# Hymba-style layer on one core: the channel mixer's sums go from GpSimd to VectorE, with new orders in its first blocks, its last token tile and its banks

## The chip, the cores and the metric

One core of one Trainium2 chip runs the whole layer as one program. The metric is the device time in microseconds (us) from launch to end; the profiled execution's span runs from the first to the last instruction. The engines are named as in the profile: PE is TensorE (matmul), DVE is VectorE, ACT is ScalarE, POOL is GpSimd, SP is SyncE, which issues nearly all DMA transfers.

## The reference

```python
def conv_glu(h, w_up, conv_w, conv_b, w_down):
    a, val = jnp.split(h @ w_up, 2, axis=-1)
    a = jax.nn.gelu(dwconv(a, conv_w, conv_b))        # depthwise, width 3, centred
    return (a * val) @ w_down
...
        x = x + g_a * (jnp.concatenate([y_m, y_a], axis=-1) @ w_out[l])
        x = x + g_f * conv_glu(modulate(rmsnorm(x, norm_ffn[l]), sh_f, sc_f),
                               w_up[l], ffn_conv_w[l], ffn_conv_b[l], w_down[l])
    return rmsnorm(x, final_norm)
```

One layer (DEPTH 1) over 1024 latent tokens of width 1024, with 256 context tokens ahead. Before the lines above come the adaLN-modulated norm, one input projection, a bidirectional mLSTM of 4 heads and windowed attention of 8 heads; the change does not touch these. The channel mixer has a width of 2816, all in fp32.

## The kernel before

Every fp32 product is split in two: an operand is copied to a rounded high part (fp32r, on ACT) and a low part is made by subtracting the high part from the operand (on DVE). A product is then three matmuls: high by high, high by low, low by high. The functions `split2`, `split`, `wsplit` and `cut` make such pairs; in the profile they are tiles such as `wh`/`wl` (up weights), `hB` (both parts of the activations, `hB[0]` and `hB[1]`), `dh`/`dl` (down weights) and `ah`/`al` (down activations).

The two large products of the channel mixer use a Strassen-Winograd form: seven block products in place of eight, at the price of sums of blocks before and after. In the up projection the activations (token halves by model halves) and each block's weights (value and gate columns by model halves) form 2 by 2 blocks. The activation sums T1 to T4 are made once, per token tile, by `sum1`, `sum2` and `sum34`. The weight sums are made for every block of 128 columns: `sums_v` makes `R[1][2]` and `R[1][3]`, `sums_g` makes `R[1][1]` and `R[1][4]`, from the four raw blocks that `load_R` brings as two transfers into Ra (2 blocks) and Rb (2 blocks and room for 3 sums).

The work in order, with the stretch of the span:

- Out-projection of the second half and the norm, up to about 683 us. Token tiles are taken in the order 1, 5, 2, 6, 3, 7, 4. `trans` turns a tile by PE into banks of the pool pT, `evac` brings it to SBUF with the modulation (tile `raw`; `er` for tile 4), and `split`, `sum1`, `sum2`, `sum34` and `split34` make the mixer's operands in `hB`. The finished x tile is stored to `x2_d` by SP.
- First products. `ps_a` (`pa`) and `ps_a2` use the weights `e0` loaded early. The five others of block 0 are `ps0` f, c, b, e, d (`pf` and so on), with `wB`, `wS`, `wA` for their weights.
- 22 blocks of the up projection (`blocks`, in pairs j and j + 11). Block 0 is made from `ps0`. For each later block PE does seven products of 12 matmuls, in the order a, b, A, c, e, d, C; A adds to the bank of a, C to the bank of c. `sn_` copies a to SBUF before A adds to its bank; `u2_`, `av2`, `av1` and `vt_` add the Winograd sums out of the banks; C can add to the bank of c when `av2` has read it. `ident_`, `taps`, `gelu` are the depthwise convolution and its activation, `mul1` (DVE) and `mul2` (POOL) the product with the value half, `combine` (POOL) the activation sums of the down projection, which SP stores to DRAM (`act_a`, `act_s`). The loop body for block i works on C = block i in PE and finishes B = block i - 1. The weights of block i + 1 are split in the meantime: `split_w(0)` to `split_w(3)` call `wsplit`, for products a/A, b/c, e/d and C. `Ra` and `Rb` have one buffer each, so their next load waits until they are read.
- Down projection: seven products m1, m6, m2, m7, m5, m4, m3 of 11 steps by 4 token tiles, the steps in pairs (`PAIRS`). `load` starts transfers four steps ahead (raw weights `br`, `b`; activations `ar`), `cut` splits them two steps ahead, and between them stand weight sums on POOL and DVE. After each product `after` adds the four results into `us`, `vs` and the output rows `os_`, one per step (`todo`).
- Tail: the last four token tiles are finished one by one and stored.

From the out-projection on, PE, DVE, ACT and POOL run their instructions in the order in which the program has them (`tc.manual_schedule`, the `fence`); SP joins after the first products (`sp_order`). Each engine takes its own list in order, so an instruction that waits holds all that stand behind it on that engine.

A helper shows its own line in the profile: `sub` is L1189, `add` L1354, `prod` L1282, the copy of `wsplit` L1377, the two halves of `split2` L1172 and L1173, `split`'s copy L1255, `dprod` L1752. So many groups share a line and are told apart by their tiles.

## Time and profile before

| | |
|---|---|
| median of 3 runs | 1367.38 us (1363.44 to 1367.88) |
| profiled execution | 1370.23 us, span 1368.4 us, mean granted PE clock 0.979 |
| busy share of the span | PE 94%, DVE 73%, ACT 44%, POOL 36% |
| DMA | 171.42 MB, mean 125 GB/s |

How to read the profile: a group is told by its line, engine, operation and tiles (out<-in), with its count, its busy time, the mean of one in ns and the idle time ahead of it with what ended that wait. The chain is followed back from the last instruction, at each step to what released it. The granted clock is what the throttle gave PE; at 0.5 a matmul of 512 columns takes 0.43 us from start to start instead of 0.23. Rows of a stretch give busy times and counts for PE, PEld (weight loads), DVE, ACT and POOL, then the clock, the DMA share and GB/s.

### The profile page before, as it was taken

What the parts mean: (1) busy time and instruction counts of PE and PEld (TensorE: products, weight loads), DVE (VectorE), ACT (ScalarE), POOL (GpSimd) and SP (SyncE); (2) the same over time, 40 slices, a digit from 0 to 9 for tenths busy, and PEclk for the clock granted to TensorE, in tenths of its full rate; (3) what the DMA queues carried; (4) which work ended last, traced back from release to release, by engine and by line L of the source; (5) the groups of instructions that cost most, each with busy time, mean ns of one, the idle gap of its engine ahead of it and who ended that gap; (6) DMA issues with size and microseconds to landing.
All of it is one profiled execution on the core that took longest, in us unless ns stands there. A gap on an engine that the chain in (4) does not pass through costs nothing.

```text
span 1368.4 us, 19850 instructions
## 1 busy us (share of the span) xinstructions
PE 1285.2 (94%) x7141; PEld 1085.3 (79%) x7141; DVE 998.1 (73%) x1736; ACT 605.7 (44%) x1195; POOL 492.9 (36%) x471
## 2 busy tenths in 40 slices
PE   6889999999898999999978999999999999899997
PEld 4689898999898777788756888777777878788786
DVE  4644787876675788996878676677667676887778
ACT  6532344444565566776644233223232333343445
POOL 0440131413445223332343444434344442535080
PEclk9999999999999999999989999999999999999999
DMA  9430443330035312212412333332332326884654
GB/s 360 150 109 32 139 143 120 121 119 5 33 98 186 134 63 84 82 67 73 156 64 77 115 94 107 100 89 88 116 100 87 114 93 222 277 314 139 223 162 154
DMA packets 86018, 171.42 MB, mean 125 GB/s; under 512 B 12672, under 2 KB 25120, under 8 KB 85920
## 3 DMA queue, kind: packets, MB, share of 16 engines
q1 hardware_dynamic: 85920, 170.16, 37.4%
q8 instruction: 56, 0.92, 0.3%
q14 instruction: 42, 0.34, 0.1%
HBM read 131.84 MB, written 38.29 MB: 124 GB/s over the span
## 4 chain that ended last, share of the span: by engine, by line
PE 27%; DVE 19%; DMA 7%; issue 7%; ACT 5%; POOL 1%; SPq 1%; ACTq 0%; DVEq 0%; POOLq 0%
PE pd L1752 9%; DVE wl L1189 4%; DMA Rb<-in_w_up_dram 3%; DMA act_s<-tt 3%; PE pa L1282 2%; PE pc L1282 2%; PE u L1069 2%; DVE tt L1472 2%; DVE tt L1474 2%; PE po L297 2%; PE pb L1282 2%; PE po L299 1%; PE po L298 1%; DVE al L1173 1%; ACT tt L1478 1%
## 5 line engine op out<-in xcount | busy, mean ns | idle before, releaser
L1752 PE MATMUL pd<-dh,al 128*128 128x512 f32 x296 | 116.5, 393 | 5.5 <-DVE al L1173 5.4
L1282 PE MATMUL pc<-hB,wh 128*128 128x512 f32 x344 | 109.4, 400 | 10.1 <-DVE av L1354 10.0
L1752 PE MATMUL pd<-dh,ah 128*128 128x512 f32 x296 | 115.9, 391 | 0.8 <-ACT ah L1172 0.8
L1752 PE MATMUL pd<-dl,ah 128*128 128x512 f32 x296 | 115.9, 392 | 0.0
L1282 PE MATMUL pa<-hB,wh 128*128 128x512 f32 x336 | 104.3, 392 | 3.9 <-ACT sn L1448 3.7
L1189 POOL TENSOR_TENSOR Rb<-Ra,Rb 128x512 f32<-128x512 f32 x44 | 71.7, 1649 | 92.4 <-DVE Rb L1354 92.3
L1189 DVE TENSOR_TENSOR wl<-Rb,wh 128x1024 fp32r<-128x1024 f32 (+1 forms) x65 | 100.0, 1587 | 6.7 <-ACT wh L1377 6.7
L1464 ACT ACTIVATE tt<-av,sp 128x1024 f32<-128x1024 f32 x22 | 27.4, 1245 | 165.5 <-DVE av L1354 62.7
L1282 PEld LDWEIGHTS pc<-hB,wh 128*128 128x128 f32 x344 | 64.2, 191 | 30.1 <-DVE av L1354 17.0
L536 PE MATMUL pp<-hl,wh 128*128 128x512 f32 x256 | 79.8, 403 | 0.0
L1282 PEld LDWEIGHTS pa<-hB,wh 128*128 128x128 f32 x336 | 62.5, 188 | 19.6 <-ACT sn L1448 6.9
L659 POOL TENSOR_SCALAR dm<-ident,mh 128x128 fp32r<-128x128 f32 x64 | 30.2, 473 | 131.7 <-PE pe L666 91.1
L297 PE MATMUL pv<-wh,hl 128*128 128x256 f32 x256 | 74.9, 292 | 0.0
L298 PE MATMUL pv<-wl,hl 128*128 128x256 f32 x256 | 72.3, 282 | 0.0
L299 PE MATMUL pv<-wh,hl 128*128 128x256 f32 x256 | 72.2, 282 | 0.0
L1752 PEld LDWEIGHTS pd<-dh,al 128*128 128x128 f32 x296 | 55.9, 189 | 18.8 <-DVE al L1173 7.4
L1484 POOL TENSOR_TENSOR tt<-vt,tt 128x512 f32<-128x512 f32 x22 | 31.0, 1407 | 108.3 <-ACT tt L1478 63.9
L1282 PE MATMUL pc<-hB,wl 128*128 128x512 f32 x172 | 67.6, 393 | 0.0
L1752 PEld LDWEIGHTS pd<-dh,ah 128*128 128x128 f32 x296 | 56.0, 189 | 12.8 <-ACT ah L1172 1.2
L1173 DVE TENSOR_TENSOR al<-ar,ah 128x1024 fp32r<-128x1024 f32 (+1 forms) x37 | 66.0, 1783 | 0.1
L1282 PE MATMUL pa<-hB,wl 128*128 128x512 f32 x168 | 65.4, 389 | 0.0
L1752 PEld LDWEIGHTS pd<-dl,ah 128*128 128x128 f32 x296 | 55.9, 189 | 12.0
(1076 smaller groups left out, 4056.6 us busy)
## 6 DMA issues: line engine op xcount, KB each, us to landing
w<-in_w_ada_dram SPq DMA_DIRECT2D x64, 256.0 KB, 2.8
br<-in_w_down_dram SPq DMA_DIRECT2D x25, 512.0 KB, 5.8
Ra<-in_w_up_dram SPq DMA_DIRECT2D x22, 512.0 KB, 3.6
Rb<-in_w_up_dram SPq DMA_DIRECT2D x22, 512.0 KB, 4.5
ar<-act_s SPq DMA_DIRECT2D x44, 256.0 KB, 3.0
act_a<-tt SPq DMA_DIRECT2D x33, 256.0 KB, 4.9
act_s<-tt SPq DMA_DIRECT2D x33, 256.0 KB, 5.1
wr<-in_w_h_dram SPq DMA_DIRECT2D x16, 512.0 KB, 4.8
```

The costliest lines, as they stand in the source:

```text
L297: T.matmul(ps, st_hi, mv_hi, start=first, stop=False)
L298: T.matmul(ps, st_hi, mv_lo, start=False, stop=False)
L299: T.matmul(ps, st_lo, mv_hi, start=False, stop=last)
L536: T.matmul(pp[:, 512 * n:512 * n + 512], wkq[sw][:, kt, cs], hl[n][part][:, kt, :], start=kt == 0 and sw + part == 0, stop=kt == KT - 1 an ...
L659: G.tensor_scalar(out=dm[:, d], in0=ident[:], scalar1=mhf[:, d, c, h:h + 1], scalar2=1.0, op0=ALU.mult, op1=ALU.mult)
L1069: T.matmul(self.u[:], vv[:, c, self.g], part[i][:, kk * 2 * P:(kk + 1) * 2 * P], start=kb + m == 0, stop=kb == last and m == 1)
L1173: V.tensor_tensor(out=lo, in0=src, in1=hi.bitcast(F32), op=ALU.subtract)
L1189: sub = lambda e, o, x, y: e.tensor_tensor(out=o, in0=x, in1=y, op=ALU.subtract)
L1282: T.matmul(ps[:], wt[sw][:, j, ks], hB[part][:, blk, kt, :], start=first and kt == 0 and sw + part == 0, stop=last and kt == 3 and sw == 1 ...
L1464: S.activation(self.tt[:], self.av[:], AF.Identity, bias=self.w(3), scale=self.w(1))
L1484: G.tensor_tensor(out=self.tt[:, h2_], in0=self.vt[:], in1=self.tt[:, h2_], op=ALU.mult)
L1752: T.matmul(ps[:], ac[sa][:, js], w[sw], start=first and n == 0, stop=last and n == 2, skip_group_check=not fresh)
```

## The change

The change has these parts.

1. Last token tile (4): it is turned in two halves with a product (`ps_a2`) between them and evacuated in two halves; its x store is issued by ACT. `split34` now copies at once and returns the subtractions; those of the last pair before it run after the norm's reciprocal.
2. First products: POOL makes all four weight sums of block 0; the split `wS` subtracts on DVE; the sums T3 and T4 of the last two tiles go from POOL to DVE and each is followed by its split.
3. Banks: pT opens on the other side, and the pool of six shared banks for b, c, e, d becomes two for f and b (`pB`) and four for c, e, d (`pC`).
4. Blocks: `sums_g` goes to DVE. Blocks 0 and 1 get an order of their own ahead of and in the first turn of the loop. In the other turns `sums_v` and `split_w(0)` stand after `u2_`, `av2` right behind them, and `sums_g`, `split_w(1)`, `split_w(2)` after `av2`, `split_w(3)` after `ident_`. The load of Ra is issued by itself ahead of that of Rb.
5. Down projection: the weight sums on POOL go to DVE, with the add one step later; the multiply-adds of `after_m2` and `after_m5` that ran on POOL go to DVE, the one of `after_m2` into a new `after_m7`.
6. Tail: the first half of the last tile's output is issued by ACT.

The diff; "..." stands where unchanged lines are left out:

```diff
 DB = 2
+RB1 = 1
 RB = 4
...
     pTk = ExitStack()
-    pT = pTk.enter_context(tc.tile_pool(name="pT2", bufs=4, space=PSUM, reuse_waits="tile"))
+    pT = pTk.enter_context(tc.tile_pool(name="pT2", bufs=4, space=PSUM, side="right", reuse_waits="tile"))
     pOk = ExitStack()
...
-    def trans(b):
+    def trans(b, kts=None):
         w = 2 if b == 4 else 4
-        pts[b] = [pT.tile([P, 4, P], F32, name="pt", tag="t") for _ in range(KT // w)]
-        if b == 4:
-            pts[b] = pts[b][2:] + pts[b][:2]
-        for kt in (4, 5, 6, 7, 0, 1, 2, 3) if b == 4 else range(KT):
+        if not kts:
+            pts[b] = [pT.tile([P, 4, P], F32, name="pt", tag="t") for _ in range(KT // w)]
+        else:
+            pts.setdefault(b, [None] * 4)
+            for i in sorted({kt // 2 for kt in kts}):
+                pts[b][i] = pT.tile([P, 4, P], F32, name="pt", tag="t")
+        for kt in kts or range(KT):
             T.transpose(pts[b][kt // w][:, kt % w], hns[b][:, kt * P:(kt + 1) * P], ident[:])
-    def evac(b):
+    def evac(b, kts=None):
         w = KT // len(pts[b])
-        raws[b] = (tbp.tile([P, 2, 4, P], F32, name="raw00") if b == 0 else
-                   er[:].rearrange("p a (k t) -> p a k t", k=4) if b == 4 else
-                   tbp.tile([P, 2, 4, P], F32, name="raw", tag=f"raw{b // 4}", bufs=2 - b // 4))
-        for kt in (4, 5, 6, 7, 0, 1, 2, 3) if b == 4 else range(KT):
+        if b not in raws:
+            raws[b] = (tbp.tile([P, 2, 4, P], F32, name="raw00") if b == 0 else
+                       er[:].rearrange("p a (k t) -> p a k t", k=4) if b == 4 else
+                       tbp.tile([P, 2, 4, P], F32, name="raw", tag=f"raw{b // 4}", bufs=RB1 if b > 4 else 2))
+        for kt in kts or range(KT):
             ga, sh = ada2[:, 16 + kt:17 + kt], ada2[:, 8 + kt:9 + kt]
...
+    def sum3(b, e=V):
+        sub(e, raws[b][:, 0], raws[b][:, 1], raws[b][:, 0])
+    def sum4(b, e=V):
+        sub(e, raws[b - 4][:, 1], raws[b - 4][:, 1], tbs[b][:, 0])
     def sum34(b):
-        sub(G, raws[b][:, 0], raws[b][:, 1], raws[b][:, 0])
-        sub(G, raws[b - 4][:, 1], raws[b - 4][:, 1], tbs[b][:, 0])
+        sum3(b, G)
+        sum4(b, G)
...
     def split34(b):
-        split(V, b, T3, 1, raws[b][:, 0:1])
-        split(V, b, T4, 1, raws[b - 4][:, 1:2])
+        parts = [(raws[b][:, 0:1], T3), (raws[b - 4][:, 1:2], T4)]
+        ts = slice(b % 4 * P, b % 4 * P + P)
+        for src, blk in parts:
+            S.copy(hB[0][:, blk:blk + 1, :, ts], src)
+        def lo():
+            for src, blk in parts:
+                sub(V, hB[1][:, blk:blk + 1, :, ts], src, hB[0][:, blk:blk + 1, :, ts].bitcast(F32))
+        return lo
...
         if late and b != last:
-            late()
+            late()()
             late = None
...
             split_t2(pp)
-        nc.sync.dma_start(x2_d[b][:], xs[b])
+        if b != last:
+            nc.sync.dma_start(x2_d[b][:], xs[b])
         if i + 2 < len(order):
...
     prod(ps_a, e0, 0, B11, True, True)
-    late()
+    lo = late()
     sq(4, 1)
     norm_b(4, True)
+    lo()
+    nc.scalar.dma_start(x2_d[4][:], xs[4])
     evac(7)
-    trans(4)
+    trans(4, (4, 5, 6, 7))
+    ps_a2 = pA.tile([P, 512], F32, name="pa2", tag="a")
+    prod(ps_a2, e0, 1, B21, True, True)
+    trans(4, (0, 1, 2, 3))
     pOk.close()
+    pB = pu.enter_context(tc.tile_pool(name="pB", bufs=2, space=PSUM, reuse_waits="tile"))
     pb_.close()
...
-    def load_R(m):
-        R = fr.tile([P, 2, 512], F32, name="Ra", tag="Ra"), fr.tile([P, 5, 512], F32, name="Rb", tag="Rb")
-        for t in range(2):
+    def load_R(m, ts=(0, 1), R=None):
+        R = R or [fr.tile([P, 2 + 3 * t, 512], F32, name=f"R{'ab'[t]}", tag=f"R{t}") if t in ts else None for t in range(2)]
+        for t in ts:
+            R[t] = R[t] or fr.tile([P, 2 + 3 * t, 512], F32, name=f"R{'ab'[t]}", tag=f"R{t}")
             nc.sync.dma_start(R[t][:, 0:2], I["w_up"][m, :, 2 * t:2 * t + 2].rearrange("p q k f -> p q (k f)"))
...
-    def sums_g(R, n):
-        if n == 0:
-            sub(G, R[1][:, 1], R[0][:, 0], R[1][:, 1])
-        else:
-            sub(G, R[1][:, 4], R[0][:, 1], R[1][:, 3])
+    def sums_g(R, e=V):
+        sub(e, R[1][:, 4], R[0][:, 1], R[1][:, 3])
+        sub(e, R[1][:, 1], R[0][:, 0], R[1][:, 1])
...
     sums_v(R, G)
-    sums_g(R, 1)
-    ps_a2 = pA.tile([P, 512], F32, name="pa2", tag="a")
-    prod(ps_a2, e0, 1, B21, True, True)
+    sums_g(R, G)
+    evac(4, range(4, 8))
+    sum1(7)
     split(V, 7, B22, 1, raws[7][:, 1:2])
-    sum1(7)
+    split(V, 4, B22, 1, raws[4][:, 1:2])
     wB = wsplit(R, 3)
-    evac(4)
-    split(V, 4, B22, 1, raws[4][:, 1:2])
+    evac(4, range(4))
     sum1(4)
-    wS = wsplit(R, 1, G)
-    S.copy(ar0[:], ps_a[:])
+    wS = wsplit(R, 1)
     split_t1(7)
     split_t1(4)
+    S.copy(ar0[:], ps_a[:])
     sum2(7)
...
     pTk.close()
-    pB = pu.enter_context(tc.tile_pool(name="pB", bufs=6, space=PSUM, reuse_waits="tile"))
-    newp = lambda pool, n, t: pool.tile([P, 512], F32, name=n, tag=t)
-    ps0 = {n: newp(pB, "p" + n, "b") for n in "fcbed"}
+    pC = pu.enter_context(tc.tile_pool(name="pC", bufs=4, space=PSUM, side="right", reuse_waits="tile"))
+    newp = lambda n: (pA if n == "a" else pB if n in "fb" else pC).tile([P, 512], F32, name="p" + n,
+                                                                    tag={"a": "a", "f": "b", "b": "b"}.get(n, "c"))
+    ps0 = {n: newp(n) for n in "fcbed"}
     prod(ps0["f"], wB, 0, B22, True, True)
...
     prod(ps0["b"], wS, 1, T2, True, True)
-    sums_g(R, 0)
-    sum34(7)
-    sum34(4)
     wA = wsplit(R, 2)
-    split34(7)
-    split34(4)
+    sum3(7)
+    sum3(4)
+    split(V, 7, T3, 1, raws[7][:, 0:1])
+    split(V, 4, T3, 1, raws[4][:, 0:1])
+    sum4(7)
+    sum4(4)
+    split(V, 7, T4, 1, raws[3][:, 1:2])
+    split(V, 4, T4, 1, raws[0][:, 1:2])
     prod(ps0["e"], wA, 1, T3, True, True)
...
         def pe(self, n):
-            if n in "ab":
-                setattr(self, n, newp(pA if n == "a" else pB, "p" + n, n))
-            elif n in "ced":
-                setattr(self, n, newp(pB, "p" + n, "b"))
+            if n in "abced":
+                setattr(self, n, newp(n))
             ps, wt, j, blk = {"a": (0, 0, B11), "b": (1, 1, T2), "A": (0, 1, B21), "c": (1, 0, T1), "e": (2, 1, T3),
...
     u2b = fs.tile([P, 512], F32, name="u2b", tag="u2")
+    B.a, B.c, B.d, B.e, B.u2c = ar0, ps0["c"], ps0["d"], ps0["e"], u2b
+    W = {0: wsplit(R, 0)}
+    C = Block(1, W, B)
+    C.pe("a")
     add(V, B.u2[:], ps0["b"][:], ar0[:])
+    sums_v(R)
     add(V, ar0[:], ps_a2[:], ar0[:])
     add(V, u2b[:], ps0["f"][:], B.u2[:])
-    B.a, B.c, B.d, B.e, B.u2c = ar0, ps0["c"], ps0["d"], ps0["e"], u2b
-    def sums(R):
-        sums_v(R)
-        sums_g(R, 0)
-        sums_g(R, 1)
-    W = {0: wsplit(R, 0)}
-    sums(R)
-    for n in range(1, 4):
-        W[n] = wsplit(R, n)
+    W[1] = wsplit(R, 1)
+    C.sn_()
+    sums_g(R)
+    B.av2()
+    W[2] = wsplit(R, 2)
+    B.av1()
+    B.ident_()
+    W[3] = wsplit(R, 3)
     R = load_R(blocks[2])
...
         last = i == NF - 1
-        C = Block(i, W, B)
+        if i > 1:
+            C = Block(i, W, B)
+            C.pe("a")
+            C.sn_()
         W = {}
-        split_w = lambda *ns: [W.__setitem__(n, wsplit(R, n)) for n in ns if not last]
-        C.pe("a")
-        if i > 1:
+        def split_w(*ns):
+            for n in ns:
+                if not last:
+                    W[n] = wsplit(R, n)
+        if i == 1:
+            C.pe("b")
+            C.u2_()
             split_w(0)
-        C.sn_()
-        if i == 1:
-            B.av2()
-            B.av1()
-            B.ident_()
+            Rn = load_R(blocks[3], (0,))
+            B.vt_()
+            B.taps()
+            B.gelu()
+            for n in "Aced":
+                C.pe(n)
+            C.av2()
+            sums_v(R)
+            C.av1()
+            split_w(1)
+            B.mul1()
+            B.mul2()
+            C.ident_()
+            sums_g(R)
+            B.combine()
+            split_w(2, 3)
+            R = load_R(blocks[3], (1,), Rn)
+            C.pe("C")
+            B = C
+            continue
         B.vt_()
         B.taps()
-        if i < 3:
-            sums(R)
-        if i == 1:
-            split_w(0)
-        C.pe("b")
         B.gelu()
...
         B.mul2()
+        C.pe("b")
         C.u2_()
-        split_w(1)
+        if not last:
+            sums_v(R)
+        split_w(0)
         C.pe("A")
         C.pe("c")
-        split_w(2, 3)
-        if i < NF - 2:
-            R = load_R(blocks[i + 2])
         if i == NF - 2:
...
             break
+        sums_g(R)
+        split_w(1)
+        Rn = load_R(blocks[i + 2], (0,)) if i < NF - 2 else None
+        split_w(2)
         C.av1()
         C.ident_()
-        if 1 < i < NF - 2:
-            sums(R)
+        split_w(3)
+        R = Rn and load_R(blocks[i + 2], (1,), Rn)
         C.pe("C")
...
         for ns in halves[::-1]:
-            nc.sync.dma_start(out[b * P:(b + 1) * P, ns], o[:, ns])
+            e = S if b == 3 and ns.start == 0 else nc.sync
+            e.dma_start(out[b * P:(b + 1) * P, ns], o[:, ns])
...
         norm1(i, 0)
-        scaled(G, tmp_()[:], us[i][:], i, 1)
+    def after_m7(i):
+        add(V, vs[i][:], Y[i][:], us[i][:])
+        scaled(V, tmp_()[:], us[i][:], i, 1)
...
         add(V, t[:], X[i][:], vs[i][:])
-        scaled(G, t[:], t[:], 4 + i, 1)
-        scaled(G, tmp_()[:], vs[i][:], 4 + i, 0)
+        scaled(V, t[:], t[:], 4 + i, 1)
+        scaled(V, tmp_()[:], vs[i][:], 4 + i, 0)
...
     after = {"m1": lambda i: S.copy(us[i][:], X[i][:]), "m6": lambda i: add(V, us[i][:], Y[i][:], us[i][:]),
-             "m2": after_m2, "m7": lambda i: add(V, vs[i][:], Y[i][:], us[i][:]), "m5": after_m5, "m4": after_m4}
+             "m2": after_m2, "m7": after_m7, "m5": after_m5, "m4": after_m4}
     products = [("m1", X, True), ("m6", Y, True), ("m2", X, False), ("m7", Y, True), ("m5", X, True), ("m4", Y, True),
...
                 wpair(rows[k], 0, 1, k)
-            if n in sums:
-                k = sums[n]
+            if n - 1 in sums:
+                k = sums[n - 1]
                 m = len(PAIRS[k])
-                sub(G, b22[k][:, 0:m], b22[k][:, 0:m], rows.pop(k)[:, 0:m])
+                add(V, b11[k][:, 0:m], b22[k][:, 0:m], b11[k][:, 0:m])
             if n + 2 in raws:
...
                 if q == "m2":
-                    sub(G, b11[k][:, 0:m], b11[k][:, 0:m], W_[:, 0:m])
+                    sub(V, b11[k][:, 0:m], b11[k][:, 0:m], W_[:, 0:m])
             if n == len(steps) - 4:
...
                 m = len(PAIRS[k])
-                add(V, b11[k][:, 0:m], b22[k][:, 0:m], b11[k][:, 0:m])
+                sub(V, b22[k][:, 0:m], b22[k][:, 0:m], rows.pop(k)[:, 0:m])
             if n == NP + 2:
```

## The prediction

> **What bounds the kernel now.** I read the page first, then the stages, then what TensorE waits for.
>
> ```profile
> span 1368.4 us, 19850 instructions
> ...
> PE 1285.2 (94%) x7141; PEld 1085.3 (79%) x7141; DVE 998.1 (73%) x1736; ACT 605.7 (44%) x1195; POOL 492.9 (36%) x471
> ```
>
> TensorE is busy nearly throughout, so a change gains only where TensorE stands still or runs at the low clock. Stages (us; busy time of PE, PEld, DVE, ACT, POOL with instructions; granted clock; DMA share; GB/s):
>
> ```profile
> 683.63:719.34 35.71, 27.04 (x100) 20.06 (x101) 28.07 (x38) 16.59 (x32) 16.11 (x10) 0.86 0.19 67
> 719.34:745.78 26.44, 20.91 (x86) 16.88 (x84) 22.56 (x21) 11.82 (x13) 9.47 (x6) 0.87 0.32 100
> 745.78:1141.74 395.96, 387.44 (x1682) 313.53 (x1680) 280.23 (x278) 124.57 (x141) 168.99 (x98) 1.00 0.32 103
> 1141.74:1361.20 219.46, 212.95 (x925) 173.98 (x923) 171.39 (x149) 90.31 (x118) 88.78 (x44) 0.99 0.63 213
> 1361.20:1368.40 7.20, 0.00 (x0) 0.00 (x0) 2.97 (x6) 2.24 (x5) 0.00 (x0) 0.83 0.54 197
> ```
>
> They are: first products and block 0; block 1; blocks 2 to 21; the down projection; the tail. The chain of the end gives the length of one undisturbed product of 12 matmuls, and two links that come back once per two blocks:
>
> ```profile
> 748.66 2.72 PE pb L1282 x12
> ...
> 879.11 7.49 DMA act_s<-tt
> 899.78 4.57 DMA Rb<-in_w_up_dram
> ```
>
> At 2.72 a product, block 1 (7 products) needs 19.0 of its 26.4: 7.4 lost. Blocks 2 to 21 (140) need 380.8 of 396.0: 15.2 lost. The down projection's 924 matmuls need 209.4 of 219.5, and its last one runs 0.4 past its slot: 9.6 lost. The first stage has 7 products (19.0) and 16 transposes (about 1.7, an estimate from the stage): 15.0 lost. In all some 47 us are to be had; nothing before 683 is touched.
>
> Who TensorE waits for, from 719 to 1142 and from 1141 on (total, times, longest), and two spells of low clock:
>
> ```profile
> PE pc L1282 <- DVE av L1354: 10.0, 10, 5.5
> PE pa L1282 <- ACT sn L1448: 3.7, 5, 2.3
> ```
> ```profile
> PE pd L1752 <- DVE al L1173: 5.4, 3, 2.5
> ```
> ```profile
> 738.00:744.80 6.80, 3.44 (x8) 2.77 (x9) 4.52 (x6) 2.17 (x2) 0.29 (x1) 0.50 0.50 142
> 1270.40:1273.80 3.40, 3.40 (x10) 2.62 (x9) 2.23 (x3) 1.99 (x2) 0.00 (x0) 0.50 0.91 292
> ```
>
> The first wait is product C, which adds to the bank that `av2` must have read; `av2` stands on VectorE behind three weight subtractions. The second is product A behind the copy `sn`. The clock halves for 3.4 us or twice that after the long waits, so a wait costs up to 1.7 or 3.4 more than itself.
>
> **The change part by part.**
>
> *First products and block 0.* Rows of the chain, the timeline and the R loads' line:
>
> ```profile
> 686.00 5.28 DMA Rb<-in_w_up_dram
> ...
> 694.12 1.26 POOL Rb L1189
> ...
> 695.41 0.62 ACT wh L1377
> ```
> ```profile
> 698.15 1.52 PE L1282 MATMUL pf<-hB,wh 128*128 128x512 f32 x2 [5.30 <-ACT hB L1255]
> ...
> 699.12 2.54 POOL L1189 TENSOR_TENSOR wl<-Rb,wh 128x1024 fp32r<-128x1024 f32 x1 [3.75 <-ACT wh L1377]
> ...
> 700.08 3.81 DVE L1189 TENSOR_TENSOR hB<-raw,hB 128x512 fp32r<-128x512 f32 x2 [0.66 <-ACT hB L1255]
> ```
> ```profile
> L1360 SPq DMA_DIRECT2D Rb<-in_w_up_dram x22: 328/333/1759, 686.0 to 1099.1; - x22
> ```
>
> Now SP issues Rb behind the store of x tile 4; three POOL sums of 1.3 follow the landing at 691.3, then the copy `wh`, and the evacuation of tile 4, queued behind that copy on ScalarE, holds pf until 698.15. New: the store goes to ScalarE's queue, so Rb's issue can move from 686.0 to as early as some 683 (the end of the out-projection, which I take to free its room); half of tile 4 is transposed and evacuated ahead of `wh`. Walking the queues with these durations, pf starts at 693.5 (696.1 if Rb is as late as now). The store costs ScalarE one issue, unseen there: by SP's row 0.33 to 1.76, and as the evacuation behind it has about a microsecond to spare I take nothing, 1.4 at most. Then the subtraction for `wl` runs on VectorE for 1.22 instead of 2.54 on POOL, the pair at 700.08 is no longer stretched (two times 0.69), and the T3 and T4 sums leave POOL: c starts near 696.5 and gets its low part at 697.8, b at 700.5, e at 703.8 (waiting 0.6 for T3), d at 707, and block 1's first product at 709.7 instead of 719.34: 9.6. With Rb late, 2.5 of it goes, and two half-clock windows would cost 3.4: 3.7 to 9.6, taken 8.0, because some forty hand-overs were walked with hardly any slack. A loss would need Rb later than now, and its issue is only moved ahead.
>
> *Block 1.* Today three subtractions stand ahead of `av2`, C waits 5.5 and then runs at half clock. New: C's `av2` stands ahead of the sums. But vt of block 0 now stands behind u2 and a weight subtraction, and the split pool gives c, d and e four banks: e of block 1 takes the bank of c of block 0, which vt must read first. My walk has vt end 1.1 after e could start, and av2 ready at C. So 19.0 + 1.1 = 20.1 instead of 26.4: 6.3. If e waits as long as C does now, with one half-clock window, 0.2 is left; without that wait 7.4. Taken 5.5.
>
> *Blocks 2 to 21.* Groups from 740 to 1120, 19 blocks (line, engine, shapes, count, busy, mean ns, idle before):
>
> ```profile
> L1189 DVE TENSOR_TENSOR wl<-Rb,wh 128x1024 fp32r<-128x1024 f32 x38 | 66.0, 1773 | 1.0 <-ACT wh L1377 1.0
> ...
> L1474 DVE SCALAR_TENSOR_TENSOR tt<-av,sp,tt 128x1023 f32<-128x1023 f32 x19 | 24.4, 1284 | 0.7
> ...
> L1354 DVE TENSOR_TENSOR Rb<-Rb 128x512 f32<-128x512 f32 x19 | 13.2, 692 | 42.1 <-DMA Rb<-in_w_up_dram 42.1
> ...
> L1354 DVE TENSOR_TENSOR u<-pb,sn 128x512 f32<-128x512 f32 x19 | 12.9, 681 | 0.2 <-PE pb L1282 0.2
> ```
> ```profile
> L1189 POOL TENSOR_TENSOR Rb<-Ra,Rb 128x512 f32<-128x512 f32 x38 | 61.7, 1643 | 75.7 <-DVE Rb L1354 75.7
> ```
> ```profile
> L1464 ACT ACTIVATE tt<-av,sp 128x1024 f32<-128x1024 f32 x19 | 23.6, 1245 | 155.2 <-POOL tt L1189 54.9 <-DVE av L1354 52.4 <-DMA act_s<-tt 47.9
> L1478 ACT ACTIVATE tt<-tt 128x1024 f32<-128x1024 f32 x19 | 20.2, 1061 | 72.5 <-DVE tt L1474 72.5
> ```
>
> And over the tiles wl and Rb, with min/median/max ns or us:
>
> ```profile
> L1189 DVE TENSOR_TENSOR wl<-Ra,wh x21: 1215/1335/2330, 716.0 to 1105.1; 128x1024 fp32r<-128x1024 f32 x21
> ```
> ```profile
> DMA to landing us min/median/max: 3.6/4.5/5.3
> ```
>
> Undisturbed, the subtraction takes 1.22; its mean of 1.77 is POOL beside it. The two POOL sums per block (3.3) become two of 0.69 on VectorE. VectorE per block: four sums 2.8, three `wl` 3.7 and the half one 0.7, two taps 2.6, six adds and products fed from a bank 4.1: 13.8. Its closed loop also waits for gelu (1.06) and, between av1 and the last `wl`, for the identity (1.25) and a copy of 0.62: 16.7 against 19.0. In the new order only one `wl` stands ahead of av2, and sums_v, which today blocks VectorE for 42.1 on the landing of Rb, comes last before it. The added wait is Rb's reload: freed by the last `wl`, 2.5 into the next block, landed 4.5 later at about 7.1 (7.9 at the maximum), wanted at 8.1; behind it stand one `wl` and av2, with 3 us to spare before C. The act_s stores that hold the identity on every second block come sooner, because POOL goes from mul2 straight to the combine. Bounds: all 15.2 gained, or (third rival) a loss; I take 13.5, which leaves under 0.1 a block.
>
> A rule that speaks against this part: the Trainium skill's SBUF — State Buffer (Who interferes with whom) has a VectorE op with two SBUF inputs and a GpSimd op that reads SBUF shut each other out for a whole instruction, so more such sums on VectorE could only swap who waits. The 2.33 maximum of a 1.22 `wl` agrees. By the rule at its worst the sum is the third rival's. What holds the loop below that is the row of u<-pb,sn: one of its inputs lies in a bank, and it keeps 681, so mul2, which runs beside such ops, costs VectorE nothing, and only sums_v and one `wl` meet the combine.
>
> *Down projection.*
>
> ```profile
> L1173 DVE TENSOR_TENSOR al<-ar,ah 128x1024 fp32r<-128x1024 f32 x31 | 57.5, 1855 | 0.1
> ```
> ```profile
> 1163.62 2.40 POOL L1189 TENSOR_TENSOR b<-b,br 128x1024 f32<-128x1024 f32 x1 [9.28 <-DMA br<-in_w_down_dram]
> 1167.71 2.42 POOL L1189 TENSOR_TENSOR b<-b,br 128x1024 f32<-128x1024 f32 x1 [1.69 <-DMA br<-in_w_down_dram]
> 1171.75 3.42 POOL L1189 TENSOR_TENSOR b<-b,br 128x1024 f32<-128x1024 f32 x1 [1.62 <-DMA br<-in_w_down_dram]
> ```
> ```profile
> 1262.84 2.31 DVE L1189 TENSOR_TENSOR br<-br 128x1024 f32<-128x1024 f32 x1
> ...
> 1267.47 2.29 DVE L1173 TENSOR_TENSOR al<-ar,ah 128x1024 fp32r<-128x1024 f32 x1
> ```
>
> TensorE's three waits of 5.4 stand behind such stretched `al`: two between 1169 and 1176, one up to 1270 with a half-clock window; short restarts make up the 9.6. VectorE takes 12 weight sums (1.22 each, two of 0.69) and 24 half-tile ops of 0.69: 30 more, and gets 31 × 0.63 = 20 back from `al` alone. Per step of 24 matmuls (5.45) it has at most 5.3, in the steps with after_m7 and after_m5, with two steps' lead. The new danger is VectorE waiting itself for the br loads, as POOL does now: subtracting where the loads landed (1163.6, 1167.7, 1171.8), `al` of step 6 ends at 1172.4 where TensorE wants it at 1172.2, so 0.5 remains there. Near 1267, two ops of 2.3 shrink to 1.2 and those before them likewise, about the lateness. Of 9.6, bounds 0 to 9.6 (below nothing only if loads come later, which an earlier `al`, freeing their rooms, argues against), taken 7.0.
>
> *Tail and the rest.*
>
> ```profile
> 1357.58 7.94 SPq L1707 DMA_DIRECT2D out_dram<-o  x8
> ```
>
> The last tile's first half leaves from ScalarE's queue and not behind SP's issue: 0 to 1 (7.94 / 8 an issue), taken 0.3. The bank pool's side and the deferred last split: 0 to 0.5 on the norm's reciprocal, inside the walk.
>
> **Sum.** 8.0 + 5.5 + 13.5 + 7.0 + 0.3 = 34.3. The profiled execution took 1370.2, so 1336; it lies 2.8 above the median of 1367.4, so 1333 by that. I say 1335.
>
> **The rivals.** *First: the opening doesn't pay.* Rb comes as late as now, two half-clock windows fall there, and e waits for vt as C does now: 3.7 + 0.2 instead of 13.5, so 1335 + 9.6 = 1345. For it: the low clock already follows gaps of a few microseconds, and the walk has gaps near 1.7. Against: tile 4's evacuation no longer hangs on the sums.
>
> *Second: the stalls of blocks 2 to 21 stay,* because the loop by way of act_s (7.49 at the longest) or Rb still closes late: 13.5 less, 1349. For: both links come back in every pair. Against: 2.3 of slack in the loop.
>
> *Third, slower: VectorE becomes the bound.* Without the sums POOL keeps (168.99 − 65)/20 = 5.2 us per block; if VectorE stood still for all of it, the loop is 16.7 + 5.2 = 21.9 against 19.8 now: 20 × 2.1 = 42 lost, less 20.8 gained elsewhere, about 1389. It decides from 20.8 a block, 4.1 of the 5.2 held. For: `wl` at 1773. Against: u<-pb,sn at 681, and that av2 waits for e anyway, which absorbs some.
>
> *Fourth: no change,* if every price fails in part.
>
> **Chances.** Forecast 0.68 (own range 1328 to 1341), first 0.11, second 0.10, third 0.06, fourth 0.05. The range 1328 to 1350 takes in the first two. Faster by over 0.3% (what a measurement of this kernel can tell: its three runs lie 4.4 us apart): 0.89; within it 0.05; slower 0.06.
>
> **What would show it.** Right: pf some 4 us earlier, C of block 1 hardly waiting, no gap between d and C or b and A from block 2 on, VectorE's `wl` and `al` near 1.22 to 1.5, POOL's sums gone. Wrong: VectorE idle before Rb sums or br for over 3 us at a time, e waiting for vt by several us, half-clock windows at the opening, or VectorE without idle time and C late in every block.

## The result, and the profile after

The changed kernel takes 1329.37 us in the median (1326.37 to 1335.63) where the kernel before, run beside it, takes 1367.63: ratio 0.9718, 95% interval 0.9657 to 0.9779. In a later comparison of five rounds it took 1328.19 against 1364.70: 0.9733 (0.9707 to 0.9758). Forecast were 1335, within 1328 to 1350, and "faster" at 0.89.

The page of the changed kernel: span, and the busy time of each engine.

```profile
span 1329.1 us, 19745 instructions
...
PE 1270.1 (96%) x7141; PEld 1082.2 (81%) x7141; DVE 1000.4 (75%) x1819; ACT 610.1 (46%) x1195; POOL 329.1 (25%) x388
```

POOL lost 164 us of work (492.9 before), and VectorE hardly gained any (998.1 before) though it issues 83 instructions more: what it took over, it got back from instructions that are no longer stretched by POOL. Its stages, cut at the first matmul of each (columns as in the table of before: length, then busy time of PE, PEld, DVE, ACT, POOL, granted clock, DMA share, GB/s):

```profile
679.39:707.86 28.47, 24.48 (x101) 18.12 (x101) 26.46 (x41) 16.29 (x31) 5.92 (x4) 0.94 0.23 84
707.86:726.95 19.09, 19.09 (x85) 15.77 (x84) 16.61 (x22) 9.62 (x10) 1.30 (x1) 1.00 0.16 56
726.95:1109.43 382.48, 381.34 (x1681) 315.17 (x1680) 293.45 (x322) 128.94 (x142) 98.37 (x61) 1.00 0.32 109
1109.43:1321.26 211.83, 210.26 (x924) 173.06 (x923) 166.93 (x185) 92.68 (x120) 12.76 (x8) 1.00 0.64 222
1321.26:1329.10 7.84, 0.39 (x2) 0.00 (x0) 3.12 (x6) 2.39 (x6) 0.00 (x0) 0.79 0.55 201
```

With the border of the last two stages at the start of the last matmul in both kernels:

| stage | before | after | gained | predicted |
|---|---|---|---|---|
| up to the first transposes (same code) | 683.63 | 679.39 | 4.2 | 0 |
| first products and block 0 | 35.71 | 28.47 | 7.24 | 8.0 |
| block 1 | 26.43 | 19.09 | 7.34 | 5.5 |
| blocks 2 to 21 | 395.96 | 382.48 | 13.48 | 13.5 |
| down projection | 218.89 | 211.83 | 7.06 | 7.0 |
| tail, to the end of the span (1368.43 and 1329.14) | 7.81 | 7.88 | -0.07 | 0.3 |

The changed stages give 35.1 against a predicted 34.3. The 4.2 of the first row are no part of the change: over the kernels below (e10b apart), this stage, the same code in all, took 675.7 to 687.7, with the low clock falling now here and now there. So the 39.3 between the two profiled spans are 35.1 of the change and 4.2 of chance. (The medians of the later comparison lie 36.5 apart.) That the total came so near its forecast is in part luck: the opening gained 0.8 less than predicted and block 1 1.8 more.

Who TensorE still waits for in the changed kernel, from 676 to 727 (the end of the out-projection, the opening and block 1), then everything behind (total, times, longest; of the first list the waits under 0.5 are left out).

```profile
PE pt L1241 <- DVE raw L1255: 1.3, 1, 1.3
PE pf L1300 <- ACT wh L1402: 1.1, 1, 1.1
PE pt L1241 <- DVE hn L1227: 0.6, 1, 0.6
PE po L298 <- DVE x L1211: 0.6, 1, 0.6
```
```profile
PE pd L1808 <- DVE al L1174: 1.2, 2, 0.6
PE pc L1300 <- DVE av L1379: 1.1, 1, 1.1
PE pd L1808 <- ACT ah L1173: 0.4, 1, 0.4
```

In 602 us TensorE now waits 2.7; the ten waits for `av` that cost 10.0 (5.5 of it in block 1) are one of 1.1, and none is left for `sn`. On VectorE itself, blocks 2 to 21, the waits are:

```profile
DVE wl L1190 <- ACT wh L1402: 36.8, 21, 1.9
DVE u L1379 <- PE pe L1300: 24.8, 19, 2.4
DVE tt L1507 <- ACT tt L1504: 23.7, 20, 1.2
```

The 42.1 on Rb's landing are gone. In their place VectorE waits 24.8 for product e, which is the good kind of wait: it stands ready before TensorE is done. The groups of the loop, from 727 to 1104 (count, busy, mean ns, idle before):

```profile
L1190 DVE TENSOR_TENSOR wl<-Rb,wh 128x1024 fp32r<-128x1024 f32 x40 | 48.8, 1221 | 2.2 <-ACT wh L1402 1.7
L1190 DVE TENSOR_TENSOR wl<-Ra,wh 128x1024 fp32r<-128x1024 f32 x19 | 34.1, 1792 | 0.0
L1190 DVE TENSOR_TENSOR Rb<-Rb,Ra 128x512 f32<-128x512 f32 x19 | 31.6, 1665 | 0.6
...
L1379 DVE TENSOR_TENSOR u<-pb,sn 128x512 f32<-128x512 f32 x20 | 13.6, 680 | 0.0
```

Two `wl` of each block run at the undisturbed 1.22 (1.77 before); the first `wl` and the second of the sums_v meet POOL's combine and take 1.79 and 1.67; the bank-fed `u` keeps 0.68. That is the collision the prediction left.

### The profile page after: what moved, and what is told of

Its sections match the earlier page's. It is cut to its first block, busy times and chain, and to the rows that moved or that the text cites. A ratio compares the mean times of both kernels' runs of the same rounds, so it can differ in the third digit from the quotient of the medians.

```text
span 1329.1 us, 19745 instructions
## 1 busy us (share of the span) xinstructions
PE 1270.1 (96%) x7141; PEld 1082.2 (81%) x7141; DVE 1000.4 (75%) x1819; ACT 610.1 (46%) x1195; POOL 329.1 (25%) x388
## 4 chain that ended last, share of the span: by engine, by line
PE 51%; DVE 8%; ACT 3%; DMA 2%; issue 1%; POOL 1%; SPq 0%; ACTq 0%; DVEq 0%; POOLq 0%
PE pd L1808 13%; PE pa L1300 8%; PE pc L1300 8%; PE pe L1300 4%; PE pb L1300 4%; PE pd L1300 4%; PE u L1070 2%; PE po L298 2%; PE po L300 1%; PE po L299 1%; DVE nm L1018 1%; PE pt L1047 1%; DVE hB L1190 1%; DMA ar<-act_s 1%; DVE wl L1190 1%
## 5 line engine op out<-in xcount | busy, mean ns | idle before, releaser
L1402 ACT CAST wh<-Rb 128x1024 fp32r<-128x1024 f32 (+1 forms) x66 | 59.5, 903 | 144.7 <-PE pd L1300 81.6
L1300 PE MATMUL pc<-hB,wh 128*128 128x512 f32 x344 | 106.2, 390 | 1.1 <-DVE av L1379 1.1
L1190 DVE TENSOR_TENSOR wl<-Rb,wh 128x1024 fp32r<-128x1024 f32 (+1 forms) x66 | 68.8, 1044 | 39.3 <-ACT wh L1402 38.8
L1300 PEld LDWEIGHTS pc<-hB,wh 128*128 128x128 f32 x344 | 64.5, 188 | 15.2 <-DVE av L1379 1.6
L1808 PEld LDWEIGHTS pd<-dl,ah 128*128 128x128 f32 x296 | 55.6, 188 | 11.7 <-DVE dl L1174 0.3
L660 POOL TENSOR_SCALAR dm<-ident,mh 128x128 fp32r<-128x128 f32 x64 | 28.5, 446 | 131.7 <-PE pe L667 91.1
L298 PE MATMUL px<-wh,hl 128*128 128x256 f32 (+1 forms) x192 | 57.5, 299 | 2.8 <-ACT kr L321 2.8
L300 PE MATMUL px<-wh,hl 128*128 128x256 f32 (+1 forms) x192 | 55.2, 287 | 1.4 <-DVE hl L294 1.4
```

The source lines that it names most:

```text
L298: T.matmul(ps, st_hi, mv_hi, start=first, stop=False)
L300: T.matmul(ps, st_lo, mv_hi, start=False, stop=last)
L660: G.tensor_scalar(out=dm[:, d], in0=ident[:], scalar1=mhf[:, d, c, h:h + 1], scalar2=1.0, op0=ALU.mult, op1=ALU.mult)
L1190: sub = lambda e, o, x, y: e.tensor_tensor(out=o, in0=x, in1=y, op=ALU.subtract)
L1300: T.matmul(ps[:], wt[sw][:, j, ks], hB[part][:, blk, kt, :], start=first and kt == 0 and sw + part == 0, stop=last and kt == 3 and sw == 1 ...
L1402: S.copy(wt[0][:], src)
```

## The experiments

Stage times are cut as in the table. Each experiment ran once, apart from e9 and the unchanged copy (e0). Where a kernel leaves a stage as the change has it, that stage shows the spread: opening 27.8 to 28.5, block 1 19.0 to 19.1, blocks 2 to 21 381.9 to 382.5, down projection 210.3 to 211.8. The one exception is e10a, whose down projection took 214.5 behind its slower loop.

**What carries blocks 2 to 21: the engine or the order?** The theory was the order, the rival the engine. e1 puts the two sums of the loop back on POOL in the new order; e2 takes the kernel before, with its order, and only moves them to VectorE, for every block from block 1 on.

```diff
 e1 (changed kernel, loop from block 2 on)
-        sums_g(R)
+        sums_g(R, G)
 e2 (kernel before)
-    def sums_g(R, n):
+    def sums_g(R, n, e=G):
...
-        sums_g(R, 0)
-        sums_g(R, 1)
+        sums_g(R, 0, V)
+        sums_g(R, 1, V)
```

> The changed kernel with one thing undone: from block 2 on, the two sums of sums_g run on POOL again; their place in the order stays. Blocks 2 to 21 took 382.5 us after the change and 396.0 before. Theory 'order': what counts is that av2 stands ahead of the weight splits and the sums behind it, so the POOL sums (3.3 us a block) only stretch the weight subtractions, inside the loop's slack of 2.3 us: 382.5 to 385.5. Rival 'engine': the 13.5 us came from POOL's sums no longer holding VectorE: 390 to 396, with the mean of the 1.22 us subtraction back near 1.75. The other stages stay within 0.3 us, apart from the granted clock.

> The kernel before with one thing done: the two sums of sums_g run on VectorE for every block from block 1 on, in the old order (all three weight subtractions ahead of av2, sums after ident). Theory 'order': C still waits for av2 behind three subtractions, only the shorter ones, and VectorE still stands before Rb's landing: blocks 2 to 21 at 390 to 396. Rival 'engine': 382.5 to 385, C's wait for av2 (10.0 us in 10 times) gone. If both this one and the run with POOL sums in the new order are near 383, each alone is enough. Opening unchanged at 35.7, down projection at 219.

e1: blocks 2 to 21 take 382.82 (382.48 after), the whole 1329.99. The sums on POOL do meet VectorE, and it doesn't matter; the groups of e1:

```profile
L1190 POOL TENSOR_TENSOR Rb<-Ra,Rb 128x512 f32<-128x512 f32 x38 | 58.4, 1556 | 5.6 <-DVE Rb L1190 5.6
L1190 DVE TENSOR_TENSOR wl<-Rb,wh 128x1024 fp32r<-128x1024 f32 x38 | 50.6, 1347 | 4.9 <-ACT wh L1402 4.5
```

e2: 392.98, so 3.0 of 13.5 gained, 1357.29 in all. TensorE's waits, and the first of VectorE's, in e2:

```profile
PE pa L1282 <- ACT sn L1448: 3.2, 3, 2.1
PE pc L1282 <- DVE av L1354: 2.9, 6, 0.6
```
```profile
DVE Rb L1354 <- DMA Rb<-in_w_up_dram: 36.6, 17, 3.0
```

The old order keeps its waits, and VectorE still stands 36.6 before Rb. So the order carries the loop: it brings 13.1 without the move from GpSimd, which is worth 3.0 alone and 0.3 on top of the order. (e1 keeps the rest of the change too; of that, e7 below excludes the banks.)

**Which part of the order?** e10a puts sums_v back to the end of a turn, ahead of the next vt, and leaves av2 ahead of the splits. e10b does the reverse: sums_v stays behind u2, and the other sums and two splits go back ahead of av2.

```diff
 e10a (and likewise at the end of block 1's turn)
         C.u2_()
-        if not last:
-            sums_v(R)
         split_w(0)
...
         R = Rn and load_R(blocks[i + 2], (1,), Rn)
+        if R:
+            sums_v(R)
 e10b
+        if not last:
+            sums_g(R)
+            split_w(1)
+            Rn = load_R(blocks[i + 2], (0,)) if i < NF - 2 else None
+            split_w(2)
         C.av2()
...
-        sums_g(R)
-        split_w(1)
-        Rn = load_R(blocks[i + 2], (0,)) if i < NF - 2 else None
-        split_w(2)
```

> After, with sums_v back at the end of a turn, ahead of the next vt (where the old order had it), and av2 left ahead of the weight splits. Theory 'the sums placed behind u2 hide Rb's landing, and this is needed': VectorE stands some 4.5 a block for Rb, wl0 ends near 15.8 into a block instead of 12, and av2 comes 0.8 later than C wants it: blocks 2 to 21 take 390 to 402 (382.5 after), VectorE's idle time before Rb 60 to 90. Rival 'only av2 ahead of the splits matters, VectorE's slack of 4 a block absorbs the landing': VectorE idles as much, but C waits at most a few times and the stage stays at 382.5 to 385.

> After, with sums_v left behind u2 and the two other sums and the splits of the sums and of Rb (two wl) moved ahead of av2, the old order's place. Theory 'av2 ahead of the splits is needed': av2, which ends 1.1 before C starts now, comes behind 1.3 of sums and 2.5 of wl that start at 911.9 in the block at 904 to 923, so it ends 0.7 late there and 1.5 to 2.5 late where POOL's combine stretches the four: blocks 2 to 21 take 395 to 415, C waiting in nearly every block. Rival 'the place of sums_v alone carries it': C waits at most a few times, the stage stays at 382.5 to 385.

e10a took 1370.77, as slow as the kernel before, and its blocks 2 to 21 take 423.35, above what either theory gave. Waits of TensorE and of VectorE in it:

```profile
PE pc L1300 <- DVE av L1379: 25.6, 15, 4.4
```
```profile
DVE Rb L1379 <- DMA Rb<-in_w_up_dram: 73.5, 19, 5.3
```

Hiding the landing is needed; that much of the theory stands. Its size was wrong (390 to 402 were expected) since I priced C's lateness in one block and not the loop. The timeline of e10a, two blocks' Rb sums and the last `wl` between them:

```profile
903.51 0.69 DVE L1379 TENSOR_TENSOR Rb<-Rb 128x512 f32<-128x512 f32 x1 [3.67 <-DMA Rb<-in_w_up_dram]
...
921.12 0.69 DVE L1190 TENSOR_TENSOR wl<-Rb,wh 128x512 fp32r<-128x512 f32 x1 [1.87 <-ACT wh L1402]
925.52 0.69 DVE L1379 TENSOR_TENSOR Rb<-Rb 128x512 f32<-128x512 f32 x1 [3.70 <-DMA Rb<-in_w_up_dram]
```

Rb's room comes free with that last `wl`, so the load starts at 921.8, and the next turn of VectorE can't start before it has landed: 18.3 of VectorE plus 3.7 of load make 22.0 in this block (21.2 in the mean of the stage), more than the 19.04 that TensorE needs. The new order loads Rb late, because the last split is late; it can do that only because sums_v stands 5.6 us behind the next vt. These two belong together.

e10b tells nothing. In its only run TensorE was slow from the first stage on, long before the changed lines (4056.27 in all): in the median a matmul of 512 columns started 0.84 after the one before it in the up projection and 0.62 in the down projection, where the changed kernel has 0.23 in both. The same group of matmuls in the changed kernel and in e10b (groups):

```profile
L1300 PE MATMUL pc<-hB,wh 128*128 128x512 f32 x344 | 106.2, 390 | 1.1 <-DVE av L1379 1.1
```
```profile
L1300 PE MATMUL pc<-hB,wh 128*128 128x512 f32 x344 | 303.1, 1011 | 0.0
```

So what av2's place alone is worth stays open.

**The down projection.** e3 puts the weight sums back on POOL (the ones that subtract into b11 and b22), e4 the scaled rows of us, vs and t.

```diff
 e3
-                    sub(V, b11[k][:, 0:m], b11[k][:, 0:m], W_[:, 0:m])
+                    sub(G, b11[k][:, 0:m], b11[k][:, 0:m], W_[:, 0:m])
...
-                sub(V, b22[k][:, 0:m], b22[k][:, 0:m], rows.pop(k)[:, 0:m])
+                sub(G, b22[k][:, 0:m], b22[k][:, 0:m], rows.pop(k)[:, 0:m])
 e4
     def after_m2(i):
...
+        scaled(G, tmp_()[:], us[i][:], i, 1)
     def after_m7(i):
...
-        scaled(V, tmp_()[:], us[i][:], i, 1)
     def after_m5(i):
...
-        scaled(V, t[:], t[:], 4 + i, 1)
-        scaled(V, tmp_()[:], vs[i][:], 4 + i, 0)
+        scaled(G, t[:], t[:], 4 + i, 1)
+        scaled(G, tmp_()[:], vs[i][:], 4 + i, 0)
```

> The changed kernel with the 12 weight sums of the down projection (b22 less rows, b11 less W) on POOL again, in the new places. The stage took 211.8 us after and 218.9 before. Theory: the two stalls at the start of the second product stood behind these sums, the stall at the fifth product behind POOL's half-tile ops: 2.5 to 4 us come back here, 214.3 to 216, all near the first and second product, and the mean of al rises from 1.22 to about 1.5. Rival 1: the weight sums carried it all: 218 to 219, with a stall at the fifth product too. Rival 2: the later add alone removed the stalls, whichever engine subtracts: 211.8 to 212.5.

> The changed kernel with the 24 half-tile multiplies and adds of the output rows (those of after_m2 and after_m5) on POOL again, where they stood before. The down projection took 211.8 us after and 218.9 before. Theory: the stall of about 3 us and the half-clock window (1.7) at the start of the fifth product come back: 215 to 217, nothing at the second product. Rival: the stall there came from lateness built up earlier, by the weight sums: 211.8 to 213.

The stage takes 217.49 in e3 and 215.08 in e4 (211.83 after): 5.66 and 3.25 given back, more together than the 7.06, so the parts overlap. e4 is as its theory had it; e3 lies between its theory (up to 216) and its first rival (from 218). Where the time goes can be read from the starts of the matmuls (2.72 for twelve when nothing holds them): e3 loses 6.5 at the turn to the second product, where the kernel before lost 4.4 and the changed kernel loses 1.1; e4 loses 3.2 at the start of the fifth, where the kernel before lost 4.7 and the changed kernel nothing. The group of `al` in the changed kernel, in e3 and in e4, and TensorE's wait in e3:

```profile
L1174 DVE TENSOR_TENSOR al<-ar,ah 128x1024 fp32r<-128x1024 f32 x31 | 37.7, 1217 | 0.1
...
L1190 DVE TENSOR_TENSOR b<-b,br 128x1024 f32<-128x1024 f32 x9 | 11.0, 1219 | 0.8 <-DMA br<-in_w_down_dram 0.8
```
```profile
L1174 DVE TENSOR_TENSOR al<-ar,ah 128x1024 fp32r<-128x1024 f32 x31 | 48.7, 1571 | 0.1
```
```profile
L1174 DVE TENSOR_TENSOR al<-ar,ah 128x1024 fp32r<-128x1024 f32 x31 | 45.4, 1465 | 0.1
```
```profile
PE pd L1808 <- DVE al L1174: 4.9, 3, 2.6
```

Here the engine counts: `al` has two SBUF inputs, POOL's work beside it stretches it (1571 and 1465 ns in the mean against 1217), and there is no slack ahead of TensorE at these steps. Of the 5.66 in e3, 3.7 are this wait (4.9 against 1.2); a spell of low clock that follows it (0.52 from 1146.0 to 1149.4) can make up the rest. Both runs keep the later add, so what that add is worth by itself was not tested.

**The opening.** e5 sends the store of x tile 4 back to SP, ahead of Rb's load. e6 takes the last T3 and T4 low parts ahead of the norm, T3 on VectorE and T4 on POOL.

```diff
 e5
-        if b != last:
-            nc.sync.dma_start(x2_d[b][:], xs[b])
+        nc.sync.dma_start(x2_d[b][:], xs[b])
...
-    nc.scalar.dma_start(x2_d[4][:], xs[4])
 e6
-        def lo():
-            for src, blk in parts:
-                sub(V, hB[1][...], src, ...)
+        def lo(es=(V, V)):
+            for e, (src, blk) in zip(es, parts):
+                sub(e, hB[1][...], src, ...)
...
-    lo = late()
+    late()((V, G))
     sq(4, 1)
     norm_b(4, True)
-    lo()
```

> The changed kernel with the store of x tile 4 back on SP, ahead of Rb's load; all else as changed. The opening (first product to block 1's first) took 28.5 us after and 35.7 before. Theory 'early Rb': Rb is issued behind the store some 4 us later, the sums on POOL end as late as before, the copy wh and pf follow: 2 to 4 us come back, 30.5 to 32.5. Rival 'collision': POOL's early sums stretch the last split (two 0.69 us subtractions took 3.47) and so hold the evacuation of tile 7; with a late Rb this stretch goes and the two cancel: 28 to 29.5. The other stages do not move by more than 0.3 us, apart from half-clock windows.

> The changed kernel with the two subtractions of the last T3/T4 split taken out of the collision: T3's runs on VectorE at once, in the time in which VectorE waits for the root, T4's on POOL ahead of POOL's sums. Opening 28.5 us after the change. Theory 'collision': the evacuation of tile 7, which waits for T3's read of the one buffer it shares, starts 2 to 2.5 us sooner, the second half of tile 4's transposes no longer waits 1.4 us, pf starts 2 us sooner: 25 to 27, the lower end if the half-clock window there goes too. Rival: the start of pf hangs on POOL's sums and the copy wh, which a POOL subtraction ahead of them delays by 1.3 us: 28.5 to 30.

The timeline of the changed kernel, around the opening's last splits and pf:

```profile
676.88 0.60 SPq L1386 DMA_DIRECT2D Rb<-in_w_up_dram  x1
...
682.67 1.29 POOL L1379 TENSOR_TENSOR Rb<-Rb 128x512 f32<-128x512 f32 x1 [8.00 <-DMA Rb<-in_w_up_dram]
...
682.67 1.57 DVE L1227 TENSOR_SCALAR hn<-x,r 128x512 f32<-128x512 f32 x1
684.17 3.47 DVE L1190 TENSOR_TENSOR hB<-raw,hB 128x512 fp32r<-128x512 f32 x2
...
686.03 1.50 ACT L1253 ACTIVATE raw<-pt,ada 128x128 f32<-128x128 f32 x4 [2.63 <-DVE hB L1190]
...
690.83 1.37 PE L1300 MATMUL pf<-hB,wh 128*128 128x512 f32 x2 [1.14 <-ACT wh L1402]
```

Rb is issued at 676.88, 2.5 ahead of the first transposes where I had taken 0.6, and that is why it collides: POOL's four sums now run beside the norm and the last split (two of 0.69 taken as 3.47), and the evacuation of tile 7 waits 2.63 for that split, whose source is its room. In e5 POOL's sums start only at 690.03, behind both, and there hn takes 0.49 and the two subtractions 1.29 together. Its opening of 30.16, with pf waiting 5.3 for `wh`, lies between theory and rival and shows that the early load is worth 1.7 to 2.4 all the same. e6 (26.94) gains 0.8 to 1.5: pf starts 8.9 us into the stage instead of 11.4, and the collision moves on, to the low parts that pf itself needs. POOL and VectorE in e6 (timeline):

```profile
687.90 3.28 POOL L1190 TENSOR_TENSOR Rb<-Ra,Rb 128x512 f32<-128x512 f32 x2
...
688.29 1.76 DVE L1190 TENSOR_TENSOR hB<-raw,hB 128x512 fp32r<-128x512 f32 x1
689.98 1.75 DVE L1190 TENSOR_TENSOR hB<-er,hB 128x512 fp32r<-128x512 f32 x1
```

The spread of the opening between runs of the same order comes from the same collision. The norm's scaling and POOL's first sum in e1 (timeline), to be set beside the two rows at 682.67 above:

```profile
683.65 0.49 DVE L1227 TENSOR_SCALAR hn<-x,r 128x512 f32<-128x512 f32 x1
...
683.73 1.55 POOL L1379 TENSOR_TENSOR Rb<-Rb 128x512 f32<-128x512 f32 x1 [8.09 <-DMA Rb<-in_w_up_dram]
```

In e1 and e7 the scaling starts 0.08 ahead of POOL's sum and takes 0.49; pf starts 10.4 into the stage, and the opening takes 27.8. In the changed kernel, e0, e3, e4, e8 and e10a the two start within 0.05 of each other and the scaling takes 1.55 to 1.62; pf starts at 11.4 to 11.5, and the opening takes 28.4 to 28.5.

**The bank split.** e7 gives the up projection one pool of six banks, as before, with all orders left new.

```diff
 e7
-    pB = pu.enter_context(tc.tile_pool(name="pB", bufs=2, space=PSUM, reuse_waits="tile"))
...
-    pC = pu.enter_context(tc.tile_pool(name="pC", bufs=4, space=PSUM, side="right", reuse_waits="tile"))
+    pB = pu.enter_context(tc.tile_pool(name="pB", bufs=6, space=PSUM, reuse_waits="tile"))
```

> The changed kernel with one pool of six banks for f, b, c, e, d opened where the four are opened now, as before the change. Theory: the split of the pool only lets f start in a bank that the out-projection left: pf starts behind the last evacuation of tile 4, up to 2 us later (opening 28.5 to 30.5), and block 1 (19.1 us) and blocks 2 to 21 (382.5) stay. Rival: with c, e, d and b in one ring of six, a block's e or c has to wait for a bank that is read late (vt, u2): blocks 2 to 21 lose 0.2 to 1 us each, 386 or more, or block 1 loses 1 us or more.

Opening 27.77, block 1 19.04, blocks 2 to 21 382.54: nothing, neither the later pf of the theory nor the rival's waits. (Its 1338.04 is due to the stage ahead of the change, 687.71.)

**A better version.** e8 does the last combine's three sums on VectorE. e9 joins e6, e8 and one more step: block 0's last pair sum leaves POOL for VectorE, just ahead of its own split.

```diff
 e8
-        def combine(self):
+        def combine(self, e=G):
...
-    C.combine()
+    C.combine(V)
 e9 = e6 + e8, and
-    sums_g(R, G)
+    sub(G, R[1][:, 4], R[0][:, 1], R[1][:, 3])
...
+    sub(V, R[1][:, 1], R[0][:, 0], R[1][:, 1])
     wA = wsplit(R, 2)
```

> The changed kernel with the three sums of the last block's combine on VectorE. The down projection took 211.8 us after the change, 2.4 of it in stalls at its steps 4 to 6. Theory: those stalls come from the raw weights (b, br), whose loads stand on SP behind the stores of that combine, which POOL finishes at 1124 next to VectorE's splits: with the sums at 0.7 us each the loads start 3 to 4 us sooner and the stalls go: 209.5 to 210.5. Rival: the loads wait for the rooms that hB and the last block's tiles leave, or for the stores to land: 211.3 to 212.3.

> After, with three things moved: the low parts of the last T3/T4 splits ahead of the norm (T3 on VectorE, T4 on POOL), block 0's second pair sum (Ra minus Rb) from POOL to VectorE just ahead of its own weight split, and the last combine's three sums on VectorE. Theory 'the opening is bound by VectorE and by what POOL's sums stretch there': in the run with the early low parts two B22 low parts of 0.69 took 1.76 and 1.75 and sum1 1.23 beside POOL's last two sums (687.90 to 691.18); with one of these gone at least the two low parts fall back to 0.69, VectorE takes 0.69 more later, so about 1.5 net: opening 25 to 26.5 (28.5 after, 26.9 with the low parts alone). Rival 'pf waits for tile 4's evacuation and the clock, not for VectorE': opening 26.9 to 28. Both: down projection 209 to 209.6, tail 8.2, blocks as after; so 3.7 to 5.5 below the unchanged copy run beside it by the first, 2.3 to 3.5 by the rival, in the sum of the stages from the first product on.

> The changed kernel unchanged, for comparison on the same chip: ratio to before 0.969 to 0.976, opening 27.8 to 28.5, down projection 210.3 to 211.8; what differs by more between runs lies before the first product, in code that is the same in both.

e8: the down projection takes 209.21, its 924 matmuls without a wait; the 2.6 that the prediction had left there are gone, and the tail is 0.4 longer. The way was the one expected. The first load of weights behind that combine's stores, in the changed kernel and in e8 (timeline):

```profile
1124.39 0.43 SPq L1653 DMA_DIRECT2D b<-in_w_down_dram  x1
```
```profile
1123.25 0.43 SPq L1653 DMA_DIRECT2D b<-in_w_down_dram  x1
```

The stage starts at 1109.43 and at 1111.58, so the load goes out 11.7 into it instead of 15.0. e9 keeps the 209.21, though its tail came out at 9.32, 1.0 above e8's, all of it behind the last computation. Its opening takes 28.91, against 26.94 with e6's part alone: theory and rival both fell. The row of e9's product e, and the windows of its half-clock spell:

```profile
697.38 0.49 PE L1300 MATMUL pe<-hB,wh 128*128 128x512 f32 x1 [1.93 <-ACT hB L1260]
```
```profile
698.60:702.00 3.40, 3.40 (x10) 2.68 (x9) 3.07 (x5) 2.17 (x3) 0.00 (x0) 0.53 0.01 4
```

One low part falls back to 0.68, and c and b start earlier than in e6 (12.4 and 16.4 into the stage against 15.1 and 17.8); but the moved sum and the `wl` that waits for its copy put off the T3 sums on VectorE, e waits 1.9 for them, and the low clock then falls on e. In all e9 takes 1327.41 (1326.29 to 1328.23), the unchanged copy on the same chip 1328.19 (1327.39 to 1330.53): ratios to before 0.9723 (0.9699 to 0.9748) and 0.9733 (0.9707 to 0.9758). That is no difference that can be told. e6 with e8 and without the moved sum, which by the stages of e6 and e8 would be 1.5 to 3.7 below the changed kernel, wasn't run.

## Why the prediction was right, point by point

*Opening, 8.0 predicted, 7.24 measured.* The way to it was half right. The early issue was (I took 683, 0.6 ahead of the first transposes; it came 2.5 ahead of them), and the store on ScalarE's queue did cost nothing. But pf started 3.1 earlier against the first transposes (11.4 into the stage, 14.5 before), not 4.65: I had walked the queues with undisturbed durations and had not asked what POOL's earlier sums would now lie beside. The scaling of hn and the last split took 5.04 there and 1.78 in e5. The other 4.1 come behind pf, as walked: 3.4 of them in product b (6.78 from its start to e's before, 3.34 after), whose wait of 2.2 for a stretched low part is gone. One half-clock spell fell on pf, where the bound had two. I had priced such a spell at 1.7; here it cost nothing that can be seen, because product c then no longer waits for its low part (in e8, without a spell, it waits 1.0, and the opening is as long).

*Block 1, 5.5 predicted, 7.34 measured.* The step that failed is "e of block 1 takes the bank of c of block 0". Block 1's e and block 0's vt in the changed kernel (tile view, timeline):

```profile
L1300 PE MATMUL pe<-hB,wh x8: 389/389/390, 718.8 to 721.1; 128*128 128x512 f32 x8
```
```profile
719.20 0.68 DVE L1379 TENSOR_TENSOR vt<-pc,u2b 128x512 f32<-128x512 f32 x1
```

e started before vt had even begun to read that bank, so it can't have waited for it, and the block runs in 19.09, which was my upper bound. I had taken the banks to go round in the order of their requests; the rows of before didn't show that, and which bank e did take no row of the changed kernel shows either. e7 adds that the number of pools makes no difference either.

*Blocks 2 to 21, 13.5 predicted and 13.48 measured*, with 1.7 left of 15.2: the one wait of 1.1 and 0.6. The parts named were the right ones (sums_v behind u2, one `wl` ahead of av2, Rb landed in time), and Rb, issued at 921.9, is in 3.6 later and wanted at 927.4, with 1.9 to spare where I had counted 1.0. What the prediction had no word for is e1: that the loop would run as fast with the sums still on POOL. The added work on VectorE was argued at length, and it was the order that mattered. The weighing against the Trainium skill's SBUF — State Buffer (Who interferes with whom) came out on the side of the bank-fed rows: `u` at 680 ns, and only the sums_v and one `wl` stretched, to 1.67 and 1.79. In e1 the two sums take 1556 ns on POOL and the `wl` from Rb 1347, as that section would have it, and VectorE's slack absorbs it.

*Down projection, 7.0 predicted, 7.06 measured*, by the mechanism named: `al` fell from 1855 ns to 1217, and e3 and e4 bring part of it back with the stalls. VectorE doesn't wait for the br loads (0.8 in all before `b<-b,br`), the danger I had named.

*Tail, 0.3 predicted, -0.07 measured.* The store of the last tile's first half on another queue brought nothing.

*The rivals.* VectorE as the bound (the slower one) needed it to stand still for 4.1 of POOL's 5.2 per block; it still waits 24.8 / 19 = 1.3 per block for product e. The stalls that stay, and the opening that doesn't pay, are excluded by the stage table.

## What to carry to other kernels

When work moves from one engine to another and changes its place in the order in the same edit, look at which of the two pays: in the loop with slack the order gave nearly all (13.1 of 13.5) and the engine 0.3; in the stage without slack, where the receiving engine's ops were being stretched, putting work back cost 3 to 6. A load into a single room closes a loop with the engine that frees it: add the load to that engine's turn before comparing with the bound (18.3 + 3.7 against 19.04), and put the first use of the load at least as far into the turn as the load is long. And where a transfer comes earlier, look at what the work it releases will then lie beside.
